# Letting the first group's state-space scan start beside the query projections of a one-core Hymba step

## The chip, the cores and the metric

The kernel runs on one core of one Trainium2 chip. The metric is device time in microseconds for one execution, from the first instruction to the last on that core. The kernel before was timed in three runs, and one further execution was recorded with the hardware profiler; its trace is what the prediction reads.

## The reference, cut to what matters

One decoder layer is computed for a prompt of 2048 tokens and for 8 single-token samples. The input projection of the normalised rows is split by columns into queries, keys, values, a gate z, the scan's inputs x/B/C, and eight step sizes dt. Attention and scan both need that one projection, and both feed the output projection:

```python
h = rms_norm(x, norm1_w)
proj = h @ w_in
q, k, v, z, xbc, dt_raw = jnp.split(proj, SPLIT_IDX, axis=-1)
a = swa_prompt(q, k, v, attn_sinks, rel_bias)          # window 128, banded blocks
s_out, new_conv, new_h = ssm_mixer(z, xbc, dt_raw, ...) # conv, chunked scan, gate, norm
x = x + jnp.concatenate([a, s_out], axis=-1) @ w_out
...
# in ssm_mixer, after the causal convolution:
y, h = ssd(xs, dt, A, B, C, h0)                         # chunks of 128 tokens
y = y + xs * D_skip
y = y * silu(z)                                         # the gate z is needed only here
```

The scan of one chunk needs x/B/C and dt. The gate z enters only after it, in the last product. A feed-forward block and a final norm follow.

## The kernel before, in words

**Tiling.** The tokens are cut into six groups of two or three blocks of 128 tokens; the first four have 384 columns. Features lie on the partitions, tokens on the free axis. Every projection unit makes 128 output features of one group: 8 slices of the contraction times 3 products (high weight with high and low input, low weight with high input, `mm3`, all through `mm` at L104), so 24 matmuls of 128x384 into one PSUM bank of the four called `psd`. Smaller products and transposes go through four banks called `psm`.

**Weights.** A unit takes two weight halves. `weight` (from L200) loads a raw half by SP's DMA queue (L208), ScalarE rounds it to the high part (L209), and VectorE subtracts to make the low part (L210); it may be stored for later groups (L216) and is then reloaded ready-made (L205). The third of a unit's matmuls already needs the low part, so TensorE can start a unit with two matmuls and then waits for L210.

**Stages.** Each stage is a generator that yields once per unit or step. For group i: X loads and normalises the input (L323 and L341 to L350 are its VectorE work), A projects dt and x/B/C and convolves (L365 to L409), K projects keys and values (L460 to L495), B projects four query units and then four gate units (L507 and L514 to L520; `take` at L316 evacuates a unit of group 0 on VectorE), P is attention block by block (L548 to L640), Q is the scan block by block (`ssd`, L708 to L772) and its norm (L670 to L680), S splits both results into high and low parts (L924, L927), O is the output projection, H the second norm, F the feed-forward.

**One scan block.** `ssd` has eight steps. It reloads the running sums of dt from DRAM, broadcast over the partitions (`big<-csd`, L713; the sums are stored by L452), multiplies C by B (`cb`, L720), takes exponentials (L723, L724, L733, L750), transposes x and B on TensorE (L731, L738), scales x (L735, L745), forms the decay matrix (L741, L760), applies the old state (L752) and updates it (L753, L761), adds the skip term (L763). Then it waits until the group's fourth gate unit exists, and only the last two steps use the gate (L771, L772).

**The order of the work.** `run(main, *rest)` steps a main stage unit by unit, and after every unit advances the side stages by a rate written by hand (steps per unit, carried as a fraction). The lines that matter say: project group 0's keys and values (K) with the normalisation of group 1 (X) beside them; then five units of B (four query units and the first gate unit) with X alone; then the remaining three gate units with attention P and scan Q beside them at 61/15 and 44/15 steps a unit; then A of group 1 with both, then seven units of B of group 1, where S of group 0 begins as soon as P and Q of group 0 have ended; then group 0's output projection O. A scheduler places the emitted instructions onto the five engines' queues by its own estimates, and each engine runs its queue in order. So the code's order sets what is ready when, and the scheduler's order is what the chip executes.

Of the kernel before, what the change touches and what calls it, by code (L numbers as in the profile page):

```python
# [14 lines left out]
ALU = mybir.AluOpType  # L15
# [6 lines left out]
U0, UB = 15, 7  # L22
# [4 lines left out]
PA, PA1 = (), ()  # L27
UQ = 5
RH0 = 3
DM = 1024  # L30
KT = DM // P
NH = 8
# [31 lines left out]
def ff_chunks(nf):  # L64

    r = [list(range(f, min(f + FC, nf))) for f in range(0, nf, FC)]
    if len(r) > 1 and len(r[-1]) == 1:
        r[-2:] = [r[-2] + r[-1]]
    return r
# [3 lines left out]
def hymba(ctx: ExitStack, tc: tile.TileContext, I: dict, O: dict, groups):  # L73
# [5 lines left out]
    chunks = ff_chunks(NF)  # L79
    c_off = [c[0] * DM for c in chunks]  # L80

# [6 lines left out]
    def T(shape, dtype=F32, tag=None, bufs=1):  # L88
        cnt[0] += 1
        nm = f"{tag}_{cnt[0]}"  # L90
        return sb.tile(shape, dtype, tag=tag, name=nm, bufs=bufs)
# [9 lines left out]
    V, S, G, PE, SP = nc.vector, nc.scalar, nc.gpsimd, nc.tensor, nc.sync  # L101
# [63 lines left out]
    def load_bias(bscr):  # L165
        for h in range(NH):
            SP.dma_start(bias[:, h, :],
                         bscr[h, 0:P * (TW - 1)].rearrange("(q w) -> q w", w=TW - 1)[:, P - 1:P - 1 + 2 * P])
# [19 lines left out]
    def tick():  # L188
        clock[0] += 1
        now = sorted((d for d in due if d[0] <= clock[0]), key=lambda d: d[:2])  # L190
        due[:] = [d for d in due if d[0] > clock[0]]
        for d in now:
            d[2]()
# [46 lines left out]
    def act_pair(home):  # L240
        return tuple(T([P, KT, NMAX], F32R, tag=home + part) for part in ("hi", "lo"))
# [27 lines left out]
    def stage_x(g):  # L269
# [8 lines left out]
        yield from squares(xr, sq, N)  # L278
        yield from rinv_b(sq, N, DM)
        yield from scaled(xr, S_N1, sq, N, x, lambda m: xr[:, m, :N])  # L280


    def stage_x0(g):
# [19 lines left out]
        for m in range(KT):  # L303
            S.activation(xr[:, m, :N], xr[:, m, :N], AF.Square)
            mm(ps[:, :N], ones, xr[:, m, :N], m == 0, m == KT - 1)
            if m % 4 == 3:
                yield
        yield from rinv_b(r, N, DM, [ps])

# [15 lines left out]
    def squares(x, sq, N):  # L325
        t = None
        for m in range(KT + 1):
            if t is not None:
                total(sq, t, N)
            t = T([P, NMAX], tag="tmp", bufs=6) if 0 < m < KT else None  # L330
            if m < KT:
                square(x, m, sq if m == 0 else t, N)
            yield

    def scaled(x, c, r, N, pair, to):

        ts = {}

        def low(m):
            e = V  # L340
            e.tensor_tensor(pair[1][:, m, :N], ts[m], pair[0][:, m, :N].bitcast(F32), ALU.subtract)  # L341

        for m in range(KT + 2):
            if m >= 2:
                low(m - 2)
            if 1 <= m <= KT:
                S.activation(pair[0][:, m - 1, :N], ts[m - 1], AF.Copy)
            if m < KT:
                ts[m] = to(m)
                V.scalar_tensor_tensor(ts[m], x[:, m, :N], col(c, m), r[:, :N], ALU.mult, ALU.mult)  # L350
            yield
# [333 lines left out]
    def rinv_b(ss, N, d, ps=None):  # L685


        ss = [s[:, :N] for s in (ss if isinstance(ss, list) else [ss])]
        if ps is None:
            ps = []  # L690
            for s in ss:
                ps.append(PS("m"))
                mm(ps[-1][:, :N], ones, s)
            yield
        v = [T([P, NMAX], tag="tmp", bufs=6)[:, :N] for _ in ss]
        for s, p in zip(ss, ps):
            S.activation(s, p[:, :N], AF.Abs_reciprocal_sqrt, bias=epsc[:, 0:1], scale=1.0 / d)
        for s, u, p in zip(ss, v, ps):
            S.activation(u, p[:, :N], AF.Copy, bias=-0.5 * EPS, scale=-0.5 / d)
        yield  # L700
        for s, u in zip(ss, v):
            V.tensor_tensor(u, u, s, ALU.mult)
            V.tensor_tensor(u, u, s, ALU.mult)
            V.scalar_tensor_tensor(s, u, 1.5, s, ALU.add, ALU.mult)
        yield

    def ssd(g, b):
        xbc, zT = g["xbc"], g["zT"]  # L708
        tk = slice(b * P, (b + 1) * P)
        hs = slice(b * NH, (b + 1) * NH)  # L710
        dt, cs = g["dt"][:, 0, hs], g["cs"][:, hs]
# [39 lines left out]
        t1 = T([P, 4, P], tag="m2", bufs=M2)  # L751
# [17 lines left out]
            mm(yd[(h % 2) * 64:(h % 2) * 64 + 64, (h // 2) * P:(h // 2 + 1) * P], xdt[:, h, :], csb[:, h, :])  # L769
        yield  # L770
        V.tensor_tensor(t1, yd.rearrange("p (a i) -> p a i", a=4), t1, ALU.add)  # L771
        V.scalar_tensor_tensor(xbc[:, 0:4, tk], t1, 0.5, zT[:, :, tk], ALU.mult, ALU.mult)  # L772
        yield


# [192 lines left out]
    def stage_h(g):  # L968
        N, x1, sq = g["N"], g["x1"], g["sq"]
        while g.get("nsq", 0) < KT:  # L970
            yield
        yield from rinv_b(sq, N, DM)
        h2 = g["h2"] = act_pair("a" if g is gs[-1] else "b")
# [66 lines left out]
    def stage_z(g):  # L1040
        N, x1, sq, off = g["N"], g["x1"], g["sq"], g["off"]
        while g.get("nsq", 0) < 2 * KT:
            yield
        yield from rinv_b(sq, N, DM)
        for m in range(KT):
# [6 lines left out]
    for nb, smp in groups:  # L1052
        g = dict(nb=nb, smp=smp, b0=b0, off=off, N=nb * P + (NS if smp else 0), prev=prev)
# [11 lines left out]
    def step(c, i):  # L1065

        if (c, i) not in made:
            made[c, i] = kinds[c](gs[i])
        return next(made[c, i], 0)

    def run(main, *rest, units=None, drain=99):


        rest = [e if isinstance(e, list) else [list(e[0]), e[1], 0.0] for e in rest]

        def advance(e, k):
            e[2] += k
            while e[2] >= 1 and e[0]:
                if step(*e[0][0]) == 0:
                    e[0].pop(0)  # L1080
                e[2] -= 1

        while units is None or units > 0:
            says = step(*main) if main else 0
            if says in (0, "tail"):
                break
            tick()
            for e in rest:
                advance(e, e[1])
            if units is not None:  # L1090
                units -= 1
        while any(e[0] for e in rest[:drain]):
            for e in rest[:drain]:
                e[2] = 0.0
                advance(e, 1)
            tick()
        return rest[drain:]

    def mixers(i, u):

        g = gs[i]
        r = [([("P", i)], (g["nb"] * 20 + 1) / u), ([("Q", i)], (g["nb"] * 9 + 17 + (60 if g["smp"] else 0)) / u)]
        return r + ([([("Y", i)], 55 / (0.8 * u))] if g["smp"] else [])
# [6 lines left out]
    r = run(("A", 0), ([("X", 1)], RX1), drain=0)  # L1110
    r = run(("K", 0), *r, drain=0)
    load_bias(bscr)
    r = run(("B", 0), *r, units=UQ, drain=0)
    r = run(("B", 0), *r, *mixers(0, U0), drain=1)
    r = run(("A", 1), *r, drain=0)
    run(("B", 1), *r, ([("S", 0)], 2), units=UB)
    run(("O", 0))
    r = run(("B", 1), ([("H", 0)], RH0), drain=0)
    run(("K", 1), *r)
    for i in range(n):  # L1120
# [4 lines left out]
        elif i + 2 < n:  # L1125
            run(("F", i), *mixers(i + 1, RM), ([("X", i + 2)], RX))
            run(("F", i))
            r = run(("K", i + 2), ([("S", i + 1)], RS), ([("Z", i)], RZ), drain=0)
# [99 lines left out]
```

## Time and profile before

| what | value |
|---|---|
| three timed runs | 2329.67, 2334.89, 2337.59 us (median 2334.89) |
| profiled execution: its own time | 2339.65 us |
| profiled execution: span from first to last instruction | 2337.9 us |
| TensorE matmul busy | 2277.3 us, 97% of the span |
| TensorE weight load busy | 2225.7 us, 95% |
| VectorE busy | 1471.7 us, 63% |
| ScalarE busy | 973.1 us, 42% |
| mean granted TensorE clock | 0.991 |

Matmul busy time is pipelined time, so 97% says that the queue is rarely empty, not that the array is at its peak. The shares are means over the whole span; the change lies in its first tenth, and what it is worth has to be read there. In the rows of a timeline a start in microseconds stands first, then the time that the row covers, engine, line, operation, output and inputs, and a count; in square brackets is the idle time ahead of it and who ended it. Where instructions follow each other without a wait, the distance from one start to the next is a little shorter than the printed duration of one, since an instruction's end overlaps the next one's start.

### The profile page before, as it was taken

The numbers are of one execution on the slowest core, as the hardware profiler recorded it, in microseconds if no ns is written. First come the engines' busy times: TensorE is split into PE (matmuls) and PEld (weight loads), VectorE is DVE, ScalarE is ACT, GpSimd is POOL, SyncE is SP. The second block draws the span as 40 slices with busy tenths as digits, with TensorE's granted clock in tenths as the row PEclk, the third lists the DMA queues.
The fourth block names the chain that finished last, engine by engine and source line by source line (L and its number), as shares of the span: only waits on it lengthen the run. The fifth ranks groups of instructions, "written<-read, shape, count | busy, mean of one in ns | idle before, by whom it ended". The sixth has DMA issues, their size and how long they took to land.

```text
span 2337.9 us, 39913 instructions
## 1 busy us (share of the span) xinstructions
PE 2277.3 (97%) x14647; PEld 2225.7 (95%) x14647; DVE 1471.7 (63%) x3310; ACT 973.1 (42%) x2112; POOL 29.4 (1%) x109
## 2 busy tenths in 40 slices
PE   8996999999999999999999999999999999999998
PEld 7995999999999999999999998999999899999997
DVE  7996778866656785553666555554734567656544
ACT  6665555644444363333324323321311354434222
POOL 1000000000000000000000000000000000000000
PEclk9997999999999999999999999999999999999999
DMA  8653565667877677788778889868877987888886
GB/s 307 230 194 131 189 212 181 215 214 238 301 277 239 214 241 240 252 288 273 260 255 288 271 274 344 293 225 264 301 242 246 328 293 241 266 277 268 273 281 205
DMA packets 227230, 592.30 MB, mean 253 GB/s; under 512 B 24323, under 2 KB 64060, under 8 KB 226892
## 3 DMA queue, kind: packets, MB, share of 16 engines
q1 hardware_dynamic: 226892, 589.56, 75.3%
q8 instruction: 116, 1.90, 0.3%
q14 instruction: 78, 0.64, 0.1%
q10 hardware_dynamic: 144, 0.20, 0.0%
HBM read 479.97 MB, written 110.21 MB: 252 GB/s over the span
## 4 chain that ended last, share of the span: by engine, by line
PE 90%; DMA 5%; DVE 3%; ACT 1%; issue 0%; SPq 0%; DVEq 0%; ACTq 0%
PE psd L104 82%; PE psm L104 6%; DMA w<-wi 2%; DMA w<-wd 1%; DMA out_yT_dram<-x 1%; DVE x L1046 1%; DMA m<-sbcd 1%; PE psm L610 1%; DMA m<-in_sssm_dram 0%; PE psm L731 0%; DMA w<-wu 0%; DMA w<-wo 0%; DMA w<-wg 0%; DVE w L210 0%; DVE big L570 0%
## 5 line engine op out<-in xcount | busy, mean ns | idle before, releaser
L104 PE MATMUL psd<-bhi,w 128*128 128x384 f32 (+1 forms) x4448 | 1102.5, 329 | 2.8 <-ACT bhi L927 2.0
L104 PEld LDWEIGHTS psd<-bhi,w 128*128 128x128 f32 x4448 | 785.3, 188 | 8.2 <-ACT bhi L927 2.3
L104 PE MATMUL psd<-blo,w 128*128 128x384 f32 (+1 forms) x2224 | 725.6, 326 | 0.0
L209 ACT ACTIVATE w<-wraw 128x512 fp32r<-128x512 f32 (+1 forms) x543 | 324.3, 601 | 536.2 <-PE psd L104 420.4
L104 PE MATMUL psd<-hc,w 128*128 128x384 f32 (+2 forms) x3168 | 513.8, 319 | 7.1 <-DMA w<-wd 6.2
L104 PEld LDWEIGHTS psd<-hc,w 128*128 128x128 f32 x3168 | 494.7, 188 | 12.8 <-DVE sq L323 3.1
L104 PE MATMUL psd<-ahi,w 128*128 128x256 f32 (+2 forms) x2272 | 488.4, 305 | 15.3 <-DMA w<-wi 12.6
L210 DVE TENSOR_TENSOR w<-wraw,w 128x512 fp32r<-128x512 f32 (+1 forms) x543 | 352.7, 652 | 119.1 <-ACT w L209 109.0
L104 PEld LDWEIGHTS psd<-blo,w 128*128 128x128 f32 x2224 | 418.6, 188 | 1.5 <-issue 0.4
L104 PEld LDWEIGHTS psd<-ahi,w 128*128 128x128 f32 x2272 | 378.0, 190 | 22.0 <-DMA w<-wi 10.3
L104 PE MATMUL psd<-alo,w 128*128 128x256 f32 (+2 forms) x1136 | 346.1, 305 | 0.0
L998 DVE TENSOR_TENSOR x<-psd,x 128x384 f32<-128x384 f32 (+2 forms) x336 | 169.3, 510 | 105.1 <-PE psd L104 104.2
L104 PEld LDWEIGHTS psd<-alo,w 128*128 128x128 f32 x1136 | 215.6, 190 | 1.2
L1005 DVE SCALAR_TENSOR_TENSOR tmp<-tmp,psd 128x384 f32<-128x384 f32 (+2 forms) x132 | 66.9, 507 | 173.9 <-ACT tmp L1019 173.6
L1019 ACT ACTIVATE tmp<-psd 128x384 f32<-128x384 f32 (+2 forms) x132 | 60.1, 455 | 248.0 <-PE psd L104 247.9
L1008 DVE SCALAR_TENSOR_TENSOR tmp<-psd,tmp 128x384 f32<-128x384 f32 (+2 forms) x132 | 67.7, 513 | 126.4 <-PE psd L104 126.1
L1009 ACT ACTIVATE hc<-tmp 128x384 fp32r<-128x384 f32 (+2 forms) x132 | 64.0, 485 | 137.0 <-DVE tmp L1008 136.2
L384 DVE SCALAR_TENSOR_TENSOR x<-tmp,cols,x 128x384 f32<-128x384 f32 (+1 forms) x144 | 81.0, 567 | 47.7 <-ACT x L406 35.0
L320 ACT ACTIVATE tmp<-x 128x384 f32<-128x384 f32 (+2 forms) x84 | 40.4, 487 | 101.8 <-DVE x L945 69.5
L323 DVE TENSOR_TENSOR sq<-sq,tmp 128x384 f32<-128x384 f32 (+2 forms) x119 | 60.5, 508 | 25.0 <-ACT tmp L320 24.1
L1013 DVE TENSOR_TENSOR hc<-tmp,hc 128x384 fp32r<-128x384 f32 (+2 forms) x132 | 67.3, 510 | 13.8 <-ACT hc L1009 13.3
L945 DVE TENSOR_TENSOR x<-psd,x 128x384 f32<-128x384 f32 (+2 forms) x48 | 24.7, 515 | 70.3 <-PE psd L104 70.0
(258 smaller groups left out, 1751.3 us busy)
## 6 DMA issues: line engine op xcount, KB each, us to landing
w<-wi SPq DMA_DIRECT2D x144, 512.0 KB, 5.4
w<-wu SPq DMA_DIRECT2D x133, 512.0 KB, 4.4
w<-wg SPq DMA_DIRECT2D x131, 512.0 KB, 4.6
w<-wd SPq DMA_DIRECT2D x144, 384.0 KB, 3.6
wraw<-in_wg_dram SPq DMA_DIRECT2D x133, 256.0 KB, 3.4
wraw<-in_wu_dram SPq DMA_DIRECT2D x131, 256.0 KB, 4.1
w<-wo SPq DMA_DIRECT2D x57, 512.0 KB, 4.8
wraw<-in_wd_dram SPq DMA_DIRECT2D x144, 192.0 KB, 3.4
```

The costliest lines, as they stand in the source:

```text
L104: PE.matmul(o, l, r, start=start, stop=stop)
L209: S.activation(hi, raw, AF.Copy)
L210: V.tensor_tensor(lo, raw, hi.bitcast(F32), ALU.subtract)
L320: S.activation(t[:, :N], x[:, m, :N], AF.Square)
L323: e.tensor_tensor(sq[:, :N], sq[:, :N], t[:, :N], ALU.add)
L384: V.scalar_tensor_tensor(acc, raw[:, j:j + NP], cwc(j, t), acc, ALU.mult, ALU.add)
L998: V.tensor_tensor(x1[:, m, :N], p[:, :N], x1[:, m, :N], ALU.add)
L1005: V.scalar_tensor_tensor(t[:, :N], t[:, :N], 1.0, pg[:, :N], ALU.add, ALU.mult)
L1008: V.scalar_tensor_tensor(t[:, :N], pu[:, :N], 0.5, t[:, :N], ALU.mult, ALU.mult)
L1009: S.activation(hh[:, 0, :N], t[:, :N], AF.Copy)
L1013: e.tensor_tensor(hl[:, 0, :N], t[:, :N], hh[:, 0, :N].bitcast(F32), ALU.subtract)
L1019: S.activation(t[:, :N], pg[:, :N], AF.Tanh, scale=0.5)
```

## The change

The scan of group 0 is put beside the first five units of group 0's B, at three steps a unit, and is carried from there into the next call. Since the gate tile does not exist yet when the scan starts, `ssd` looks it up at the place of use and no longer at its head.

```diff
 UQ = 5
 RH0 = 3
+RQ = 3
...
     def ssd(g, b):
-        xbc, zT = g["xbc"], g["zT"]
+        xbc = g["xbc"]
...
-        V.scalar_tensor_tensor(xbc[:, 0:4, tk], t1, 0.5, zT[:, :, tk], ALU.mult, ALU.mult)
+        V.scalar_tensor_tensor(xbc[:, 0:4, tk], t1, 0.5, g["zT"][:, :, tk], ALU.mult, ALU.mult)
...
-    r = run(("B", 0), *r, units=UQ, drain=0)
-    r = run(("B", 0), *r, *mixers(0, U0), drain=1)
+    r = run(("B", 0), *r, ([("Q", 0)], RQ), units=UQ, drain=0)
+    r = run(("B", 0), r[0], *mixers(0, U0), drain=1)
```

In the second call `r[0]` keeps X alone, and `mixers` names Q again: the generator is the same one, so it goes on where it stood, at 44/15 steps a unit as before. The wait for the fourth gate unit inside `ssd` is untouched. So within the five units the first block can make six of its eight steps, and blocks 1 and 2 of the scan can not begin there. The instructions are the same ones in the same number. One line is inserted near the top, so a line of the kernel before has a number one higher in the changed kernel from there on.

On VectorE, this is the stretch of the kernel before that follows the norm factor of group 1 (`sq_436`) and ends with the low weight part `w_166`, which the second gate unit needs; `vs` belongs to the values, `kT`/`m` to attention's keys, `xr` to the normalisation of group 1.

```order
L704 SCALAR_TENSOR_TENSOR sq_436<-tmp_715,sq_436 128x384
L210 TENSOR_TENSOR w_161_913<-wraw_914,w_161_913 128x512
L484 TENSOR_TENSOR vs_699<-m_129_704,vs_699 128x6x64
L556 TENSOR_TENSOR m_177_996<-kT_647,m_176_995 64x128 x2
L350 SCALAR_TENSOR_TENSOR xr_380<-xr_380,cols_68,sq_436 128x384 x6
L316 TENSOR_TENSOR tmp_853<-psd_828,m_17_93 128x384
L350 SCALAR_TENSOR_TENSOR xr_380<-xr_380,cols_68,sq_436 128x384 x2
L556 TENSOR_TENSOR m_177_996<-kT_647,m_176_995 64x128
L484 TENSOR_TENSOR vs_699<-m_130_707,vs_699 128x6x64
L556 TENSOR_TENSOR m_177_996<-kT_647,m_176_995 64x128
L210 TENSOR_TENSOR w_166_952<-wraw_953,w_166_952 128x512
```

In the changed kernel the same stretch of VectorE's queue begins, after the same norm factor, with the head of the scan's block 0.

```order
L721 TENSOR_TENSOR m_141_777<-psm_774,cst_63 128x256
L485 TENSOR_TENSOR vs_699<-m_129_704,vs_699 128x6x64
L727 TENSOR_TENSOR ssm_782<-big_772,cs_593 128x8
L728 COPY ssm_782<-big_772 128x8
L736 TENSOR_TENSOR m_145_791<-psm_785,dt_363 128x512
L351 SCALAR_TENSOR_TENSOR xr_380<-xr_380,cols_68,sq_436 128x384 x7
L485 TENSOR_TENSOR vs_699<-m_130_707,vs_699 128x6x64
L351 SCALAR_TENSOR_TENSOR xr_380<-xr_380,cols_68,sq_436 128x384
```

It goes on there with the second weight half of the first gate unit (`w_174`) and ends with the low weight part of the second gate unit, which is called `w_179` here.

```order
L211 TENSOR_TENSOR w_174_968<-wraw_969,w_174_968 128x512
L742 TENSOR_SCALAR big_772<-big_772,cs_593 128x128 x5
L342 TENSOR_TENSOR alo_379<-xr_380,ahi_378 128x384 x2
L742 TENSOR_SCALAR big_772<-big_772,cs_593 128x128 x3
L746 TENSOR_TENSOR m_154_851<-m_145_791,ssm_782 128x512
L753 TENSOR_TENSOR m_156_859<-psm_853,m_142_779 128x512
L754 TENSOR_TENSOR state_79<-state_79,ssm_782 128x512
L317 TENSOR_TENSOR tmp_908<-psd_883,m_17_93 128x384
L342 TENSOR_TENSOR alo_379<-xr_380,ahi_378 128x384 x2
L317 TENSOR_TENSOR tmp_953<-psd_928,m_17_93 128x384
L342 TENSOR_TENSOR alo_379<-xr_380,ahi_378 128x384 x4
L211 TENSOR_TENSOR w_179_1007<-wraw_1008,w_179_1007 128x512
```

Before, `w_166` is the first weight part behind the eight L350 of the normalisation, and the L341 stand behind it. Now all eight of those (L342), fifteen instructions of the scan (L721, L727, L728, L736, eight L742, L746, L753, L754) and two evacuations (L317) stand ahead of `w_179`; attention's L556 has moved behind it.

On TensorE, this is the place of the kernel before where the second gate unit (`psd_963`) begins after the first (`psd_918`); `psd_1049` is the third gate unit.

```order
L104 MATMUL psd_918<-bhi_81,w_161_913 128x384
L104 MATMUL psd_963<-bhi_81,w_166_952 128x384
L104 MATMUL psd_963<-blo_82,w_166_952 128x384
L104 MATMUL psd_1049<-bhi_81,w_187_1038 128x384
L104 MATMUL psd_1049<-blo_82,w_187_1038 128x384
L104 MATMUL psd_963<-bhi_81,w_166_952 128x384 x2
```

The same place in the changed kernel has the first gate unit as `psd_973`, the second as `psd_1018` and the third as `psd_1086`; the first two matmuls of `psd_1018` stand a little earlier in the queue.

```order
L105 MATMUL psd_973<-bhi_81,w_174_968 128x384
L105 MATMUL psm_862<-m_154_851,m_153_849 128x256 x2
L105 MATMUL psd_1086<-bhi_81,w_194_1075 128x384
L105 MATMUL psd_1086<-blo_82,w_194_1075 128x384
L105 MATMUL psd_1018<-bhi_81,w_179_1007 128x384 x2
L105 MATMUL psd_1018<-blo_82,w_179_1007 128x384
```

The state product of the scan's block 0 (`psm_862`) has come in here, and the two products with C, the two transposes of x and B and the product with the old state stand further ahead in the query units. Behind these rows the `psd_1018` unit runs on, and its first matmul that is not one of its first two needs the low part of `w_179`.

On SP's queue the reload of the dt sums (L713, `big`) had seven rows between it and their store (L452) before; in the changed kernel there are two.

```order
L453 DMA csd_597<-csT_595 24x128
L217 DMA wi_169_927<-w_167_922 128x1024
L209 DMA wraw_1014<-in_wi_dram 128x512
L714 DMA big_772<-csd_597 128x1024
L209 DMA wraw_1076<-in_wi_dram 128x512
```

So the reload follows the store almost at once, and the raw weights of the third and fourth gate units come behind it.

## The prediction

> **What bounds the kernel now.** I read the page first, for the engine that ends last.
>
> ```profile
> PE 90%; DMA 5%; DVE 3%; ACT 1%; issue 0%; SPq 0%; DVEq 0%; ACTq 0%
> ```
>
> The chain that ended last is TensorE (PE) for 90%. A change elsewhere pays only where PE waits. So next comes PE's list of waits from 60 to 230 us, which holds the change and the start of group 0's output projection O.
>
> ```profile
> PE psm L610 <- ACT big L605: 17.0, 1, 17.0
> PE psd L104 <- ACT bhi L927: 2.0, 1, 2.0
> PE psd L104 <- ACT x L406: 1.0, 1, 1.0
> PE psm L104 <- DVE m L556: 0.7, 1, 0.7
> PE psd L104 <- ACT qT L507: 0.6, 1, 0.6
> ```
>
> Five waits (columns: microseconds in all, times, longest). The two longest belong to one place: PE has run out of projections and waits for group 0's attention on its third block, then for its split. The next view, of stretches, says what fills the time there (a stretch, its length, and the columns of the second line; DVE is VectorE, ACT ScalarE, PEclk the granted clock).
>
> ```profile
> core 0 of [0], span 2337.9 us
> core 0: us, PE busy (x) PEld busy (x) DVE busy (x) ACT busy (x) POOL busy (x), PEclk, DMA share, GB/s
> 75.00:95.00 20.00, 20.00 (x117) 19.29 (x116) 19.77 (x42) 14.07 (x29) 0.00 (x0) 1.00 0.57 193
> 160.00:180.00 20.00, 18.86 (x111) 16.93 (x111) 13.80 (x26) 14.28 (x34) 0.70 (x2) 1.00 0.52 172
> 180.00:216.00 36.00, 17.11 (x80) 13.53 (x78) 28.65 (x71) 22.89 (x58) 1.94 (x3) 0.72 0.37 124
> 216.00:222.00 6.00, 5.10 (x20) 4.99 (x21) 2.25 (x5) 1.76 (x4) 0.00 (x0) 0.72 0.01 3
> ```
>
> In 75 to 95 us, where the change puts the scan, PE is busy all 20 us and VectorE 19.77 of 20. There is no free VectorE time to move work into. PE stands still only from 190 on, and the chain of waits shows how it gets there.
>
> ```profile
> 72.98 22.57 PE psd L104 x130
> 95.55 1.34 PE psm L104 x12
> 96.89 0.44 PE psm L731 x4
> ...
> 101.14 0.24 PE psm L738 x2
> 101.39 0.89 PE psm L104 x8
> ...
> 106.27 1.89 PE psm L104 x20
> ...
> 216.90 13.11 PE psd L104 x65
> ```
>
> Up to about 180 us the chain is PE's own queue. Then it crosses to VectorE and ScalarE (the scan's norm, attention's third block) and returns to PE at 216.90. So the time of O's first matmul is what this change can move, and whatever holds PE up before 180 comes out there too.
>
> **The change part by part.** Nothing is added or taken away; the scan's first block is brought forward past work of VectorE, ScalarE, PE and SP. Prices are distances from start to start in these VectorE rows.
>
> ```profile
> 75.45 0.69 DVE L210 TENSOR_TENSOR w<-wraw,w 128x512 fp32r<-128x512 f32 x1
> 76.05 0.55 DVE L484 TENSOR_TENSOR vs<-m,vs 128x384 fp32r<-128x384 f32 x1
> 76.52 0.57 DVE L556 TENSOR_TENSOR m<-kT,m 64x128 fp32r<-64x128 f32 x2
> 77.13 3.26 DVE L350 SCALAR_TENSOR_TENSOR xr<-xr,cols,sq 128x384 f32<-128x384 f32 x6
> 80.31 0.55 DVE L316 TENSOR_TENSOR tmp<-psd,m 128x384 f32<-128x384 f32 x1
> ...
> 83.14 0.69 DVE L210 TENSOR_TENSOR w<-wraw,w 128x512 fp32r<-128x512 f32 x1
> ...
> 90.96 1.41 DVE L554 TENSOR_TENSOR big<-hc,big 64x512 fp32r<-64x512 f32 x2
> ...
> 97.30 0.42 DVE L720 TENSOR_TENSOR m<-psm,cst 128x256 f32<-128x256 f32 x1
> 97.64 0.68 DVE L735 TENSOR_TENSOR m<-psm,dt 128x512 f32<-128x512 f32 x1
> 98.24 2.14 DVE L741 TENSOR_SCALAR big<-big,cs 128x128 f32<-128x128 f32 x8
> ...
> 107.50 1.13 DVE L763 SCALAR_TENSOR_TENSOR m<-x,cols,m 128x128 f32<-128x128 f32 x4
> ```
>
> A 128x512 operation costs 0.60 (75.45 to 76.05), a plain 128x384 one 0.47 (76.05 to 76.52), an L350 0.53 (3.18 for six).
>
> *The second gate unit's weight.* In the kernel before, the low part is ready at 83.14 + 0.69 = 83.8. PE does 130 projection matmuls in 22.57 us, 0.1736 each; the unit's third matmul is the 72nd of that run, so it comes at 72.98 + 71 x 0.1736 = 85.3. Slack 1.5 us, and no wait there. In the changed kernel VectorE's queue is the same up to 75.45, and then holds, ahead of the end of `w_179`: L721 0.34; two L485 0.94; L727 and L728 0.2 together (128x8, an estimate under every price shown); the four 128x512 of the scan (L736, L746, L753, L754) 2.4; eight L351 4.2; eight L342 and two L317 4.7; eight L742 2.1; two weight parts 1.2 and 0.1 for the last one's end. Sum 16.2, so 91.7. PE meanwhile has 3.0 us more in front of it: the products with C 0.45 (four of the twelve in 1.34), transposes 0.44 and 0.24, the old state 0.89, the state product 0.95 (half of 1.89): 85.3 + 3.0 = 88.3. PE waits **3.4 us**.
>
> *Attention's first scores.* Behind `w_179` stand two weight parts 1.2, an evacuation 0.47, L761 twice and L762 1.8, L764 1.1, L555 twice 1.4, L557 four times 1.1: 98.8. From 91.7 PE has 22 + 12 matmuls, 5.9 us, so it asks at 97.6. Another **1.1 us** (1.2, less semaphore grain). Before, L554 was done at 92.4 and the scores began at 95.55.
>
> *Waits that go or move.* The 1.0 us behind ACT L406 goes: in the changed order ScalarE evacuates that bank ahead of the eight scalings L606 instead of behind them. The 0.6 us behind L507 goes at the second query unit, since two small products now stand between, and returns at the third, which has nothing between: nothing. **-1.0 us.**
>
> *The norm's sum.* PE makes two products for the scan's norm, and VectorE's work on their result stands ahead of attention's last steps in its queue. Counted in projection matmuls, the first of them moves from place 769 to 778: 9 x 0.1736, **+1.6 us**.
>
> *ScalarE and SP.* The exponentials move with the block; ScalarE is 14.07 of 20 busy there, so they cost nothing while PE waits for VectorE; without that cover the five of them that come forward would cost some 0.6 each, VectorE's price for that size, 3.0 us. The reload L714 moves past five transfers (four raw weights and one store); what it can cost is a rival.
>
> Sum: 3.4 + 1.1 - 1.0 + 1.6 = **+5.1 us** at O's first matmul. From 216.90 on the orders differ in buffer names and a few swaps of neighbours, and PE bounds the rest, so it is carried to the end. Span 2337.9 + 5.1 = 2343.0; the profiled execution's own 2339.65 becomes 2344.8. That execution is 4.8 above the median of the runs, so for the median 2334.89 I predict 2340.0. The price of a wait that PE did not have before is bounded below by nothing (if VectorE drains faster) and above by the whole 7.9 us by which the weight part moves, from 83.8 to 91.7; I take 3.4, since PE's row gives its arrival.
>
> **The rivals.**
>
> *The wait also cools the clock (+6.8).* After its 2.0 us gap PE ran 216 to 222 at a mean clock of 0.72, which cost 6.0 x 0.28 = 1.7 us; the 1.0 us gap inside 160 to 180 left 1.00. A gap of 3.4 us is above both: 5.1 + 1.7, so 2341.7. Against it: the gap before the slow rows came close behind the 17.0 us one. The Trainium skill (TensorE: Matmul & The Clock Gate, "What's actually happening") has the clock at half after one idle window of about 3.4 us, in windows that run freely. By that rule a gap of this length falls just at the edge; the trace agrees that a gap slows the clock, but its slow stretch came after only 2.0 us, so not with the length. Chance 0.2.
>
> *The reloaded sums come late (slower).* The mechanism is the store and reload through DRAM, now back to back, at the head of both VectorE's and ScalarE's queues.
>
> ```profile
> 68.42 0.32 SPq L452 DMA_DIRECT2D csd<-csT  x1
> 70.47 0.35 SPq L216 DMA_DIRECT2D wi<-w  x1
> ```
>
> The landing times of transfers that read or write those sums, from the view of their tile:
>
> ```profile
> DMA to landing us min/median/max: 3.7/5.4/6.6
> ```
>
> The reload can issue at about 71.3 (behind a store at 70.47 and one load). Landing in 3.7 to 6.6 us gives 75.0 to 77.9; L727 asks at 75.45 + 0.34 + 0.47 = 76.3. If the store itself needs 3.7 us to land, the reload starts at 72.4 and ends as late as 79.0: 2.7 us in which VectorE's queue (the weight parts among it) stands, all added to PE's wait: 5.1 + 2.7 + 1.7 for the clock = 9.5, so 2344.4. It decides from a landing later than about 78.2 (7.0 us slower, with no cooling). For it: store and reload share one queue with 256 KB and 512 KB transfers. Against it: the median lands at 76.7. Chance 0.17.
>
> *PE's wait is absorbed (0).* If attention's third block is bound by VectorE's total work and not by PE's arrival, O starts where it did: 2335. For it: VectorE does the same work before O, and stands idle for part of 160 to 180 (busy 13.80 of 20). Against it: in the chain, VectorE's waits there end on PE. Chance 0.17.
>
> *The idle VectorE time is filled (faster).* A scan block done early leaves less for 160 to 180, where VectorE has 6.2 us free; if all of that closes and PE's wait does not arise, O starts up to 6.2 us sooner: 2328.7. Against it: in 75 to 95 VectorE has 0.23 us free, so a block brought in there pushes something out, and that is a weight. Chance 0.12.
>
> **How the numbers follow.** My forecast has the remaining 0.34. A measurement of this kernel can tell about 0.3%, 7.0 us, from no change (the three runs lie 7.9 us apart). The forecast is under that, as are the cooled case alone and the absorbed one; scatter of the runs puts part of these above it: 0.07 of the forecast's, 0.06 of the cooled case's, 0.12 of the late reload's, so slower 0.25. The filled case is faster by more than 7.0 only with scatter: 0.09, with 0.02 from the absorbed one 0.11. Same 0.64. The range runs from 2329 (the full filled case) to 2347 (the late reload with scatter); what is left out is either of them with the scatter that adds to it.
>
> **What the changed profile would show.** Right: a wait of PE of about 3.4 us for L211 near 88 us, one of about 1 us for L557 near 98, no wait for L407 near 170, and O's first matmul near 222. Cooling: a clock below 1.00 in the slices from 88 to 96. Late reload: VectorE idle ahead of L727, released by DMA. I am wrong if PE shows no wait before 160, or if it does and O still starts at 217 or earlier.

## The result and the profile after

| | kernel before | changed kernel |
|---|---|---|
| median of 11 runs each | 2334.89 us (2329.67 to 2337.59) | 2341.49 us (2336.76 to 2349.40) |
| ratio | | 1.0028, 95% interval 1.0016 to 1.0040 |
| profiled execution, span | 2337.9 us | 2341.1 us |
| start of group 0's output projection O | 216.90 us | 223.44 us |

The change costs 6.5 us (2334.89 x 0.0028; 3.7 to 9.3 by the interval). The chain that ended last is TensorE's as before:

```profile
PE 89%; DMA 6%; DVE 3%; ACT 1%; issue 1%; SPq 0%; DVEq 0%; ACTq 0%
```

PE's list of waits from 60 to 230 us, changed kernel:

```profile
PE psm L611 <- ACT big L606: 18.1, 1, 18.1
PE psd L105 <- DVE w L211: 3.2, 1, 3.2
PE psd L105 <- ACT bhi L928: 2.0, 1, 2.0
PE psd L105 <- ACT qT L508: 0.6, 1, 0.6
PE psd L105 <- DVE tmp L317: 0.6, 1, 0.6
PE psm L105 <- DVE m L557: 0.5, 1, 0.5
```

Two rows are new: 3.2 us for a low weight part and 0.6 for an evacuated bank. The row for L406 (L407 here) is gone. The long wait did not shrink, it grew by 1.1. The stretches that the prediction read in the kernel before, with 95 to 115 added:

```profile
core 0: us, PE busy (x) PEld busy (x) DVE busy (x) ACT busy (x) POOL busy (x), PEclk, DMA share, GB/s
75.00:95.00 20.00, 16.19 (x88) 15.12 (x87) 19.19 (x45) 15.00 (x30) 0.00 (x0) 0.91 0.23 74
95.00:115.00 20.00, 20.00 (x125) 18.37 (x124) 16.08 (x52) 9.88 (x33) 0.38 (x2) 0.92 0.94 332
160.00:180.00 20.00, 19.42 (x123) 18.21 (x122) 15.51 (x34) 15.02 (x43) 0.70 (x2) 1.00 0.65 210
180.00:216.00 36.00, 17.39 (x93) 15.29 (x91) 27.11 (x68) 23.77 (x57) 1.68 (x3) 0.78 0.44 146
```

In 75 to 95 PE lost 3.8 of its 20 us, and its clock, 1.00 there before, is 0.91 and 0.92 in the first two rows. VectorE was nearly as full as before (19.19 us and 19.77), with other work. The place itself, in three rows of VectorE's and three of PE's timeline:

```profile
77.45 0.17 DVE L727 TENSOR_TENSOR ssm<-big,cs 128x8 f32<-128x8 f32 x1 [0.81 <-DMA big<-csd]
90.18 1.95 DVE L342 TENSOR_TENSOR alo<-xr,ahi 128x384 fp32r<-128x384 f32 x4
92.05 1.89 DVE L211 TENSOR_TENSOR w<-wraw,w 128x512 fp32r<-128x512 f32 x3
```

```profile
89.01 0.42 PE L105 MATMUL psd<-bhi,w 128*128 128x384 f32 x1 [0.57 <-DVE tmp L317]
92.79 0.69 PE L105 MATMUL psd<-bhi,w 128*128 128x384 f32 x1 [3.20 <-DVE w L211]
...
223.44 0.79 PE L105 MATMUL psd<-bhi,w 128*128 128x384 f32 x3 [1.96 <-ACT bhi L928]
```

The subtraction for the second gate unit starts at 92.05, behind the scan's block and the normalisation, and PE goes on when it is through. VectorE lost 0.81 us of that to the reload of the sums. The O start is 223.44 - 216.90 = 6.5 us later, and the distance is 6.5 again at 1804 us (1804.49 and 1810.97, the same feed-forward matmul in both). On the way there it is 6.4 to 6.6 until 1014 us and then 3.7 to 6.5. By the end of these two executions it is 3.2 us: behind 1804 the kernel before waited longer for reloaded feed-forward weights (`w<-wd`, 4.3 us against 2.2). The first experiment shows scatter of this size between single executions of equal queues; the median of the runs has the 6.5.

What the scan got for its early start, in VectorE's rows of its three gate products (the last operation of a block), kernel before and changed kernel:

```profile
111.09 0.69 DVE L772 SCALAR_TENSOR_TENSOR x<-m,hc 128x512 f32<-128x512 f32 x1
148.18 0.68 DVE L772 SCALAR_TENSOR_TENSOR x<-m,hc 128x512 f32<-128x512 f32 x1
162.42 0.68 DVE L772 SCALAR_TENSOR_TENSOR x<-m,hc 128x512 f32<-128x512 f32 x1
```

```profile
114.78 0.69 DVE L773 SCALAR_TENSOR_TENSOR x<-m,hc 128x512 f32<-128x512 f32 x1
148.24 0.69 DVE L773 SCALAR_TENSOR_TENSOR x<-m,hc 128x512 f32<-128x512 f32 x1
167.39 0.69 DVE L773 SCALAR_TENSOR_TENSOR x<-m,hc 128x512 f32<-128x512 f32 x1
```

Block 0 begins five units sooner and ends 3.7 us later: its last two steps wait for the fourth gate unit, which PE's lost time has pushed back. Nothing came sooner.

### The profile page after: what moved, and what is told of

The parts are those of the page before. It is cut to its first block, busy times and chain, and to the rows that moved or that the text cites. A ratio compares the mean times of both kernels' runs of the same rounds, so it can differ in the third digit from the quotient of the medians.

```text
span 2341.1 us, 39918 instructions
## 1 busy us (share of the span) xinstructions
PE 2278.3 (97%) x14647; PEld 2224.9 (95%) x14647; DVE 1472.9 (63%) x3310; ACT 974.0 (42%) x2112; POOL 29.5 (1%) x109
## 4 chain that ended last, share of the span: by engine, by line
PE 89%; DMA 6%; DVE 3%; ACT 1%; issue 1%; SPq 0%; DVEq 0%; ACTq 0%
PE psd L105 82%; PE psm L105 6%; DMA w<-wi 2%; DMA out_yT_dram<-x 1%; DMA w<-wu 1%; DMA w<-wd 1%; DMA m<-sbcd 1%; PE psm L611 1%; DMA w<-wo 1%; DVE x L1047 1%; DMA w<-wg 0%; PE psm L732 0%; DVE w L211 0%; DVE xr L351 0%; DVE x L999 0%
## 5 line engine op out<-in xcount | busy, mean ns | idle before, releaser
L211 DVE TENSOR_TENSOR w<-wraw,w 128x512 fp32r<-128x512 f32 (+1 forms) x543 | 352.6, 653 | 121.6 <-ACT w L210 113.2
```

The costliest lines, as they stand in the source:

```text
L211: V.tensor_tensor(lo, raw, hi.bitcast(F32), ALU.subtract)
```

## The experiments

All ratios are to the kernel before, run on the same chip in the same rounds. A start of O is also given net: PE's first half-speed stretch at the head of the program ended at 9.4 to 17.1 us, depending on the execution, so executions already differ from that of the kernel before by up to 2.9 us behind the 200th projection matmul (the next one starts at 52.28 in the kernel before); that lead is taken off. So counted, the changed kernel's O is 6.2 later.

### The look-up alone

```diff
-    r = run(("B", 0), *r, ([("Q", 0)], RQ), units=UQ, drain=0)
-    r = run(("B", 0), r[0], *mixers(0, U0), drain=1)
+    r = run(("B", 0), *r, units=UQ, drain=0)
+    r = run(("B", 0), *r, *mixers(0, U0), drain=1)
```

> Only the later look-up of the gate tile is kept; the scan stays where the kernel before has it, and every engine's queue is the same, row for row. Theory A (the wait at the second gate unit is the cause): nothing of it is here, so the ratio to the kernel before is 1.000 within 0.002, PE has no wait for a low weight part before 160 us, and the output projection starts at 216.9 within 0.5. Theory C (the loss sits behind 230 us, in transfers of reloaded weights that scatter from run to run): the ratio is 1.000 too, but the waits for reloaded weights behind 1000 us, 20 us in the profile of before and 15 in that of after, differ from before's by several us although the queues are equal.

Ratio 1.0002 (0.9993 to 1.0012), no wait of PE before 160 but the 0.6 us for L508 that the kernel before has too (L507 there), O at 217.88, net +1.0 with equal queues: an early place is good to about 1 us, not to the 0.5 that Theory A gave. Against the trace of before, the same matmul is up to 6.8 us later at 1498 us and 1.7 us earlier at 2271. So scatter behind 230 us can be as large as the whole effect within one execution, and it averages out. This run fits both theories; what speaks against Theory C as the cause is that the 6.5 us stand at O already, ahead of 230, and the next run, which leaves the code behind 230 as it is and takes the price away.

### The second gate unit's low parts on GpSimd

```diff
-        V.tensor_tensor(lo, raw, hi.bitcast(F32), ALU.subtract)
+        (G if name == "wi" and at[0] == T_Z + 1 and (name, at) not in seen else V).tensor_tensor(lo, raw, hi.bitcast(F32), ALU.subtract)
```

> The changed kernel, but the two low weight parts of the second gate unit of group 0 are subtracted on GpSimd and not at the end of VectorE's queue. Theory A (PE's 0.6 + 3.2 us wait at that unit and the half clock behind it, 2.6 us, are carried to the output projection): no wait for L211 near 90, clock 1.00 from 75 to 115, the output projection starts at 217 within 1 (223.4 in the changed kernel) and the time falls by about 6 us, to that of the kernel before. Theory B (VectorE's amount of work ahead of attention's third block sets that start, PE's wait is beside it): the wait goes too, but the start stays at 222 or later and the time within 2 us of the changed kernel's. If a subtraction on GpSimd lasts over 6 us, the wait stays and the run tells nothing.

Ratio 1.0004 (0.9996 to 1.0013): the price is gone but for what the interval leaves. PE's waits from 75 to 115:

```profile
PE psd L105 <- DVE w L211: 1.8, 1, 1.8
PE psd L105 <- DVE tmp L317: 0.8, 1, 0.8
```

The wait did not vanish: it went on to the third gate unit, whose low part is the next in the full VectorE queue. The clock stayed 1.00 from 75 to 115. O started at 217.26, of which 2.35 us are this execution's early lead; net it is +2.7, against 2.6 us of wait. Theory A holds in the time, in the clock and in what PE's wait is worth at O, and was wrong that the wait would go; Theory B falls. That O was back at 217 as expected is half luck.

### PE kept busy in the wait

```diff
+        [mm(ps[:, :N], w[0][0], x[0][:, 0, :N], True, True) for _ in range(fill)]
```

The count `fill` is 18 at the second gate unit of group 0 and 0 everywhere else. Each repeat is overwritten by the next product.

> The changed kernel, but the first matmul of the second gate unit is issued 18 times more ahead of its real one (3.1 us of TensorE work that is thrown away), so that PE is busy while it waits for the low weight part. The order of VectorE's work ahead of that part is the same. Theory A1 (the half clock is a part of the price, 5.3 us at half = 2.6 us): the wait for L211 shrinks from 3.2 to about 0.1, the clock stays 1.00 through 91 to 98, and the output projection starts at 220.8, 2.6 before the changed kernel's, with more TensorE work. Theory A2 (only the late weight counts, the clock does not matter downstream): the start stays at 223.4 within 0.5, or goes later by the filling.

The waits shrank to 0.7 and 0.6 us, the clock stayed 1.00 from 75 to 115, and O started at 221.79 (net +4.9), 1.65 before the changed kernel's, with 3.1 us of useless work in front of it. That is between the two theories' numbers and on A1's side. In time it shows nothing: 1.0036 (1.0020 to 1.0052) overlaps the changed kernel's 1.0028. So the half clock is shown in the trace, and a gain from covering it is not.

### Three of block 0's steps early

```diff
-RQ = 3
+RQ = 0.6
```

> The changed kernel with 0.6 scan steps a unit in place of 3, so that three of block 0's eight steps are made beside the first five units (sums reloaded, C times B, exponentials, transposes, x scaled; not the decay matrix and not the old state). By VectorE's queue the second gate unit's low parts stand behind 8.8 and 13.6 us of work from 75 us on, and not behind 16.2 and 16.8. Theory A: they are ready at about 84 and 89, PE asks at 86 to 88 and 88 to 90, so at most 1 us of wait, clock 1.00, output projection at 217 to 218, time within 3 us of the kernel before. Theory B (scan work done early is worth something to VectorE later): the output projection starts before 216. Theory D (any scan work ahead in those units costs, by PE's products and the reload): start at 220 or later without a wait at the gate unit.

Ratio 1.0008 (0.9998 to 1.0018), O at 217.89, net +3.9. PE's one early wait is another than expected, for ScalarE's rounding of a weight:

```profile
PE psd L105 <- ACT w L210: 1.8, 1, 1.8
```

Behind it stood 3.4 us of half clock. Theory A is right on the time and too low on the wait, which it had at 1 us at most and without a half clock. That O stands at 217.89, in its range, is luck: this execution has a lead of 2.9 us. B (before 216) falls, and D (late without a wait) isn't needed, since wait and half clock make 3.5 of the 3.9.

The four executions and the changed kernel's together, in microseconds:

| run | PE waits 75 to 115 | lost to half clock | filling | sum | O start, net | ratio |
|---|---|---|---|---|---|---|
| look-up alone | 0 | 0 | 0 | 0 | 1.0 | 1.0002 |
| low parts on GpSimd | 2.6 | 0 | 0 | 2.6 | 2.7 | 1.0004 |
| three steps early | 1.8 | 1.7 | 0 | 3.5 | 3.9 | 1.0008 |
| PE kept busy | 1.3 | 0 | 3.1 | 4.4 | 4.9 | 1.0036 |
| changed kernel | 3.8 | 2.6 | 0 | 6.4 | 6.2 | 1.0028 |

The half clock's loss is half of the time that PE ran in it (92.79 to 98.06, and 87.95 to 91.37). The sum gives the start of O within 1 us in every row, the scatter of the first: what PE loses before 115 arrives at O nearly whole in these kernels. (In the four kernels with an early scan the 1.0 us wait for L407 is gone too, and the wait for L606 is 1.1 longer; the two nearly cancel.)

### Letting the scan through

```diff
-        while g.get("nz") != 4:
-            yield
         yd = PS("m")
...
-        V.tensor_tensor(t1, yd..., t1, ALU.add)
-        V.scalar_tensor_tensor(xbc[:, 0:4, tk], t1, 0.5, g["zT"][:, :, tk], ALU.mult, ALU.mult)
+        V.tensor_tensor(xbc[:, 0:4, tk], yd..., t1, ALU.add)
+        if g.get("nz") == 4 or b == g["nb"] - 1:
+            while g.get("nz") != 4: yield
+            # ... a loop that multiplies the gate into every block not yet gated
```

Three kernels: with the scan where the kernel before has it, with 0.6 and with 3 steps a unit.

> The scan starts where the kernel before has it, but no longer waits for the fourth gate unit ahead of its seventh step: each block's sum is kept without the gate, and the gate is multiplied in once it exists. The operations and their number stay. Theory E (block 0's wait for the gate is what keeps an early scan from ending early): without an early start the wait hardly binds, since attention's and the scan's steps are spread over the same units; the third block's scores stay at place 824 of the projection matmuls, the output projection starts at 217 within 1.5, ratio 1.000 within 0.002. Rival F (the gate wait costs by itself): start before 214.

Ratio 1.0000 (0.9991 to 1.0009), O at 214.13 with a lead of 2.8, so net 0.0, and the waits of the kernel before. The gate's wait does not bind where the scan starts late.

> The same without the gate's wait, and with the scan of block 0 begun at 0.6 steps a unit beside the first five units. By the queues the norm of the scan stands at place 679 of the projection matmuls and not at 778, and the third attention block's scores at 762 to 782 and not behind 824. Theory E: VectorE and ScalarE work on the third block while PE still has projections, the 18 us wait for L606 shrinks by 5 to 10 us, the output projection starts at 207 to 213 and the ratio to the kernel before is 0.996 to 0.999. Rival G (VectorE's amount of work ahead of the third block decides, wherever its scores stand): start at 216 to 220 and ratio 1.000 or above; PE then waits sooner, in 110 to 180.

Ratio 0.9997 (0.9986 to 1.0008), O at 216.84, net +0.4. Theory E's wait did shrink, from 18.1 to 7.0, but O did not come at its 207 to 213: Rival G's waits came in its place.

```profile
PE psm L611 <- ACT big L606: 7.0, 1, 7.0
PE psd L105 <- ACT x L407: 5.6, 1, 5.6
PE psm L105 <- DVE m L746: 2.9, 1, 2.9
PE psd L105 <- ACT bhi L929: 2.0, 1, 2.0
PE psd L105 <- ACT w L210: 1.7, 1, 1.7
```

> The changed kernel (three scan steps a unit) without the gate's wait, so that all three blocks of the scan can run beside the first five units. In VectorE's queue the second gate unit's low parts stand behind 16.3 and 20.2 us of work, the third's behind 22.8, and attention's first scores behind 37.0 (26.6 in the changed kernel). Theory A: the wait for low weight parts near 90 grows from 3.2 to 6 to 10 us in all, with the half clock behind it, and no scan is left later: the third block's scores stand at place 790. The two roughly cancel: output projection at 219 to 227, ratio 1.001 to 1.005. Rival F (an early scan pays once it is let through): start before 215, ratio under 0.999.

Ratio 1.0002 (0.9993 to 1.0011), O at 218.26, net +1.6: between the two theories, and 5 us before the changed kernel's. The wait near 90 was no longer than in the changed kernel, where Theory A had 6 to 10. The last gate product comes 37 us sooner:

```profile
130.40 0.69 DVE L773 SCALAR_TENSOR_TENSOR x<-x,hc 128x512 f32<-128x512 f32 x1
```

```profile
PE psm L611 <- ACT big L606: 4.6, 1, 4.6
PE psd L105 <- ACT x L407: 3.4, 2, 3.2
PE psm L105 <- ACT m L551: 3.4, 2, 3.1
PE psd L105 <- DVE w L211: 3.3, 1, 3.3
```

So the early start pays once it is let through, about enough to give back the wait for the weight. It does not win: Rival F falls.

### More steps a unit, and room on VectorE

```diff
-U0, UB = 15, 7
+U0, UB = 13, 7
```

> The kernel before with attention's and the scan's steps spread over 13 units and not 15; nothing of the change. By the queues the norm stands at place 679 to 680 and not at 769. Theory E (what counts is how many projection matmuls are left when the third block of attention comes to its scores): the wait for L605 shrinks by 5 us or more, output projection at 207 to 214, ratio 0.996 to 0.999. Rival G (VectorE is full from 75 to 160 and pays each earlier step back with a late weight part): waits of PE for low weight parts between 95 and 160 that add up to what is won, start at 216 or later, ratio 1.000 or above.

Ratio 0.9997 (0.9989 to 1.0006), O at 216.30. The wait for L605 fell to 3.9, and others came:

```profile
PE psm L104 <- DVE m L745: 5.1, 1, 5.1
PE psm L610 <- ACT big L605: 3.9, 1, 3.9
PE psm L104 <- DVE big L760: 2.8, 1, 2.8
```

Rival G holds in time, but not in kind: the new waits are for the scan's own steps (L745, L760) and not for low weight parts. Two things in the traces would explain why O stays at 216 to 218 in these kernels; neither was changed alone, so they are not shown to be the cause. VectorE is busy 123.4 of the 141 us from 75 to 216 both in the kernel before and in the one let through with 0.6 steps (the five stretches of the view of stretches added up). And several waits cool the clock several times, while in one long wait most of the half clock falls where nothing runs: PE's busy time for 75 to 216 is 120.4 us in the kernel before and 125.6 in the one with 13 units, for nearly the same matmuls (721 and 723), with clocks of 0.92, 0.84 and 0.91 from 115 to 160, 160 to 180 and 180 to 216.

Taking work off VectorE was the next try, with the low parts of that whole part of the program on GpSimd, on the kernel before, on the changed kernel, and with 13 units:

```diff
+        (G if 30 <= len(seen) < 64 else V).tensor_tensor(lo, raw, hi.bitcast(F32), ALU.subtract)
```

> The kernel before, with the subtractions of the low weight parts from the second gate unit of group 0 to the end of its output projection on GpSimd, where one lasted 1.57 us in the earlier run, in place of VectorE (0.60 from start to start). 27 of them, 16 us of VectorE's 123 between 75 and 216, leave VectorE; five of them, 3 us, stand in its stretch from 183 to 201 ahead of attention's third block. Theory G (VectorE's amount of work between 75 and the output projection sets that start, wherever PE's waits fall): the wait for L605 shrinks by 3 us or more, the output projection starts at 207 to 214, ratio 0.996 to 0.999. Theory A alone (PE's queue sets it): a start at 217 and ratio 1.000, as PE's only early waits are 2 us. Rival H (GpSimd slows VectorE or is itself late): VectorE's 128x512 rows lengthen over 0.69 us, or PE waits for L210 from GpSimd; ratio above 1.001.

> The changed kernel with the same subtractions on GpSimd. If the price of the change is only that its scan pushes low weight parts back in a full VectorE queue (Theory A), the change costs nothing here: no wait for L211 over 1 us near 90, clock 1.00, output projection within 1.5 us of that of the same edit on the kernel before, ratio within 0.001 of it. If an early scan is worth something once VectorE has room (Theory I), it starts 2 us or more sooner than that. If the price is elsewhere (reload, PE's own products ahead), it is 3 us or more later.

> The kernel before with attention and scan spread over 13 units and with the low parts on GpSimd. Theory G: with 16 us less on VectorE the 12.5 us that PE waited in 110 to 180 and at L605 for VectorE's steps shrink by more than half, output projection at 203 to 210, ratio 0.994 to 0.998, and it beats both kernels. Rival K (the chain of dependent steps of one attention block, PE, ScalarE and VectorE in turn, is the limit and not the amount of work): start at 213 or later, ratio 0.999 or above, with VectorE idle for over 30 of the 141 us.

All three are slower: 1.0028 (1.0018 to 1.0038), 1.0046 (1.0032 to 1.0060), 1.0030 (1.0018 to 1.0042); O at 224.08, 227.21 and 220.69. Rival H holds, and Theory G could not be tried in this way. With 13 units PE's longest wait is another one, 5.7 us for a reloaded weight (`w<-wi`), and VectorE is idle 18 of the 141 us, not the over 30 of Rival K, so that run settles nothing about K. VectorE's groups from 75 to 217 us of the kernel before, and then with the low parts on GpSimd:

```profile
L384 DVE SCALAR_TENSOR_TENSOR x<-tmp,cols,x 128x384 f32<-128x384 f32 x24 | 14.6, 612 | 0.6 <-ACT x L406 0.4
L350 DVE SCALAR_TENSOR_TENSOR xr<-xr,cols,sq 128x384 f32<-128x384 f32 x8 | 4.4, 610 | 0.0
L624 DVE TENSOR_TENSOR m<-psm,m 128x512 fp32r<-128x512 f32 x6 | 4.1, 683 | 3.1 <-ACT m L622 3.1
```

```profile
L384 DVE SCALAR_TENSOR_TENSOR x<-tmp,cols,x 128x384 f32<-128x384 f32 x24 | 18.3, 775 | 2.2 <-ACT x L406 2.0
L350 DVE SCALAR_TENSOR_TENSOR xr<-xr,cols,sq 128x384 f32<-128x384 f32 x8 | 7.5, 999 | 0.0
L624 DVE TENSOR_TENSOR m<-psm,m 128x512 fp32r<-128x512 f32 x4 | 2.7, 682 | 0.0
```

Operations that take both inputs from SBUF got longer (610 to 999 ns, 612 to 775), and so did L741 with one tensor and two columns from SBUF (340 to 465); those with one from PSUM did not (683, 682). On the changed kernel the same edit leaves no wait for L211 near 90, as Theory A said, but O is 3.1 us later (net 4.4) than with the edit on the kernel before, so its statement on the time fails, and the later start is the one that the expectation gave to a price elsewhere. Counted as in the table, PE lost 6.4 us there between 75 and 115 (3.0 waiting, for L555 and L746, and 3.4 to half clock), and 3.5 with the edit on the kernel before (1.8 and 1.7). So most of the difference is lost in the same stretch, behind other VectorE work than the weight. With VectorE's durations changed everywhere, why isn't settled.

### Projections in the long wait

```diff
-U0, UB = 15, 7
+U0, UB = 15, 8
```

> The kernel before with all eight units of group 1's B ahead of group 0's output projection (seven before); nothing of the change. The eighth unit is 24 matmuls, 4.2 us, that stand in PE's queue between the third block's scores and L610. Theory G (PE stands still there only because VectorE and ScalarE work through attention's third block, so any ready projection is free there): the wait for L605 falls from 17.0 to about 13, the output projection starts within 1.5 us of 217, and the end comes up to 4.2 us sooner, ratio 0.998 to 1.000, as that unit is no longer to be done later. Rival L (the eighth unit was the cover of group 0's second norm behind the output projection): PE waits 3 us or more for the norm or for the first feed-forward or key units behind 250 us, ratio 0.999 to 1.002, nothing won.

Ratio 1.0014 (1.0004 to 1.0023). The wait for L605 fell only to 15.7, and in 240 to 280, where PE was busy all 40 us before, it now lost 3.1 (1.6 and 0.5 of it for the two parts of the normalised rows, L341 and L347) and ran at 0.91:

```profile
240.00:280.00 40.00, 36.89 (x203) 35.60 (x202) 29.58 (x68) 23.19 (x43) 0.29 (x1) 0.91 0.43 143
```

Rival L holds: the eighth unit was the cover of group 0's second norm. No kernel that was run beats the kernel before.

## Why the prediction was right, point by point

**The second gate unit's weight** (+3.4). Measured 3.20, with the arrivals near the forecast ones: PE asked at 89.6 (forecast 88.3), and the part was there at 92.7 (91.7). Of the later arrival, 0.8 is VectorE's wait for the reload. A wait of 0.57 for an evacuation two matmuls ahead was not in the sum.

**The clock** (a rival, +1.7 beside the sum, chance 0.2). It came, and cost 2.6. The forecast of 2340.0 left it out; the rival's 2341.7 is next to what was measured, 2341.49, but its parts are not the measured ones, and the interval of 3.7 to 9.3 us can't tell the two. It is the trace that shows the half clock, in one execution; the timed runs have no trace. My reason against it, that the earlier slow stretch stood close behind a 17 us gap, was wrong: a short gap is enough if it falls right (below).

**Attention's first scores** (+1.1). No such wait: PE came to them at 101.20, since it ran at half speed until 98.06, while VectorE was done with the last L557 at 99.9. Two terms of the sum, the scores and the clock, shared the same microseconds.

**Waits that go** (-1.0). The wait behind L406 went, and the one behind L507 stayed, as forecast.

**The norm's sum** (+1.6). The term was mis-sized. The first of the two products in the kernel before and in the changed kernel:

```profile
176.37 0.81 PE L104 MATMUL psm<-tmp,cst 128*128 128x384 f32 x2
183.27 0.81 PE L105 MATMUL psm<-tmp,cst 128*128 128x384 f32 x2
```

It started 6.9 later, while projection 769 came 4.1 later (176.72 and 180.78). That is a slip of 2.8 against the projections around it. I priced nine projection matmuls and left out the attention products between them: in the kernel before, places 769 and 778 are 3.2 us apart. At O 1.4 us came in behind the projections (last point), near the 1.6; that they come from this slip was argued and not tried.

**The reload** (late by up to 2.7, chance 0.17). VectorE did wait for it, 0.81 us here and 1.90 in the run with two low parts on GpSimd. It was a small term of the wait here and not the case of its own that I made of it.

**Absorbed, or filled.** Neither happened, but the experiments say where they would have: most of PE's wait is absorbed once the scan is let through (net +1.6 with a 3.3 us wait). That the block could not end before the fourth gate unit stood in the text ahead of the prediction; I didn't draw from it that there was nothing to win at O.

**The sum.** The terms came to 5.1, and the start of O moved 6.5 (6.2 net). PE's last projection matmul ahead of O, before and after:

```profile
187.95 0.34 PE L104 MATMUL psd<-ahi,w 128*128 128x384 f32 x1
193.06 0.34 PE L105 MATMUL psd<-ahi,w 128*128 128x384 f32 x1
```

That is 4.8 net: 3.8 for the two waits and 2.6 for the clock, less 1.0 for the wait that went; 0.6 less than these make is not placed. From there to O another 1.4 came in, where the prediction had 1.6 for the norm. That the distance is carried to the end holds without a break until 1014 us in the two traces, and for the end in the medians. So the mechanism of the forecast was right: a late weight part in a full VectorE queue, a wait of PE of the forecast length, and its way to O. That the total came within 1.5 us is in part luck: 2.6 for the clock were left out, and 1.1 for the scores that did not come were counted in.

## What to carry to other kernels

Work that is brought forward must be able to end sooner: look for the wait inside it before costing the rest. In a stretch where the in-order engine is full, what comes in pushes out what stands behind it, and if that feeds the bounding engine, price the gap and the cooled clock behind it together. Several short gaps can cost more than one long one, since each may cool the clock for work that follows (125.6 us of busy PE against 120.4 above).

## What the runs showed of the hardware

**A gap cools the clock by where it falls.** In the traces the granted clock changes only at steps of 3.41 us. Cut at those steps, the changed kernel's trace, then that with three steps early, then that with two low parts on GpSimd (first the PE busy time, later the granted clock):

```profile
87.82:91.24 3.42, 1.21 (x5) 0.49 (x3) 3.42 (x8) 1.45 (x4) 0.00 (x0) 1.00 0.00 0
91.24:94.65 3.41, 1.86 (x6) 1.86 (x7) 3.41 (x7) 1.01 (x3) 0.00 (x0) 0.50 0.35 91
94.65:98.06 3.41, 3.41 (x12) 3.41 (x11) 3.35 (x9) 0.38 (x1) 0.00 (x0) 0.50 1.01 298
```

```profile
84.54:87.95 3.41, 1.60 (x9) 1.28 (x8) 3.35 (x9) 2.42 (x4) 0.00 (x0) 1.00 0.38 92
87.95:91.37 3.42, 3.42 (x13) 2.82 (x12) 3.39 (x9) 1.59 (x2) 0.00 (x0) 0.50 0.95 346
```

```profile
91.74:95.15 3.41, 1.84 (x10) 1.84 (x11) 3.41 (x7) 0.89 (x2) 0.00 (x0) 1.00 0.54 160
95.15:98.56 3.41, 3.41 (x21) 2.76 (x21) 3.30 (x10) 0.53 (x1) 0.00 (x0) 1.00 1.03 344
```

A step in which PE is busy 1.21 or 1.60 us is followed by half clock, one with 1.84 at full clock is not; 1.86 us at half clock (0.93 of work) is. In all fourteen traces, from the first change to full clock to 10 us before the end, there are these steps in which PE is busy less than 3 us: all 118 with a busy time, multiplied by the clock, under 1.55 us are followed by half clock, 245 of 247 with more than 1.70 by full clock, and the ten between go both ways. At half clock this does not decide everything: of 57 steps in which PE was busy at least 3.3 us, 49 are followed by full clock and 8 by half. So one wait of 1.8 us cooled the clock in one execution, and waits of 0.8 and 1.8 did not in another. The Trainium skill (TensorE: Matmul & The Clock Gate, "What's actually happening") has a free-running window of 3413 ns, which the steps agree with; that a window need not be idle, only busy for less than about half at full clock, is what these rows add.

**GpSimd slows VectorE.** In the run with two low parts on GpSimd, three L351 that overlapped them lasted 1.31 us on average (0.61, 1.67 and 1.65) and the other five 0.61; one low part took GpSimd 1.57 us where VectorE's rows are 0.60 apart. The Trainium skill (SBUF — State Buffer, "SBUF: two separate sides") has the two engines share a port pair that one holds for a whole instruction, for VectorE operations with two SBUF inputs among others; the rows agree, and the ones with a PSUM input that kept their 683 ns do too.
